# A new order for the mixer steps of a decoder block, other GpSimd work, and 512-column products for w_glu and w_out

## Chip, cores and metric

The kernel runs on one core of one Trainium2 chip. The metric is device time in microseconds (us) from the start to the end of one execution, as the median of several runs. The five engines of the core work from queues of their own, each in its own fixed order: TensorE (PE in the profile; PEld is its weight load), VectorE (DVE), ScalarE (ACT), GpSimd (POOL) and SyncE (SP, which here issues the DMAs).

## What is computed

One layer over 256 positions of 2048 features, batch 1, float32:

```
xn   = rmsnorm(x, norm1_g);  proj = xn @ w_in              # 2048 x 3072
u    = conv4(proj[:, :1024]) ; gate = proj[:, 1024:2048] ; s = proj[:, 2048:]
r, i = sigmoid(u @ w_a + b_a), sigmoid(u @ w_i + b_i)      # 16 heads of 64
a    = exp(-8 r softplus(-lam))
y_rg = gelu(gate) * scan(a, sqrt(1 - a^2) * i * u)         # h_t = a_t h_(t-1) + b_t
z    = gelu(s5(s))            # 64 groups of 16 features, 64 complex states each, a linear scan
y_s5 = z * sigmoid(z @ w_glu + b_glu)                      # 1024 x 1024
x    = x + [rmsnorm(y_rg) ; rmsnorm(y_s5)] @ w_out         # 2048 x 2048
g, v = split(conv3(rmsnorm(x) @ w_up))                     # 2048 x 12288
out  = rmsnorm(x + (gelu(g) * v) @ w_down)                 # 6144 x 2048
```

## The kernel before

Features lie on the 128 partitions and the 256 positions along the free dimension, so each weight matrix is cut into columns of 128 outputs and loads of 512 KB, 128 rows by 8 blocks of 128x128. TensorE multiplies each block with a 128x256 tile of activations.

**Three forms of product.** `product_whole` multiplies the float32 weights as they are; the 24 columns of w_in use it, and the trace shows two matmul instructions of 256 columns for each block. `product` splits every weight into a high and a low part (`part`: a cast on ScalarE, L150, and a subtraction on VectorE, L151) and every activation too (`split`, L198 to 208), and adds three of the four partial products. In its narrow form a block takes three matmuls of 256 columns (L158, L159, L160). In its wide form the two that share the high weights are one matmul of 512 columns (L156) into both halves of a PSUM bank, and `total` afterwards adds the halves: a copy on ScalarE (L166) and an addition on VectorE (L167). The letters in `WIDE` say which products are wide; before it is "FD", which is the feed-forward part except the last output column. The 8 products of w_glu and the 32 half products of w_out, 8 blocks each, are narrow.

**The mixer steps.** `ORDER` is a hand-written list of steps, a letter and an index each, traced in that order:

- U j, P j, B g, G j are the RG-LRU group: product and causal convolution; gates; one batch of four j (exp, tanh, sqrt, and the products of L685 and L686); gate product, scan (L692), gelu and split of the output. P writes its gates into one buffer `tau` per batch, of which there is one.
- S c, T c, K c, N c, Y c, F c, Z c are the S5 group: product; tables of cosines and sines (six instructions, L505 to 507); matrices (six instructions for `ball`, L525 to 527, eight for `cp`, L534 to 538, transposes on TensorE and eight small DMAs issued by SyncE); the scan, some 7 us of VectorE; the output matmuls (L599 to 607); gelu; split.
- W o and E o are the RG half of an output column of w_out and its addition to the residual on GpSimd, L o a column of w_glu, V o the S5 half of w_out with the residual sum, its square (added up on GpSimd) and the split. R, Q and a last call make the three norm factors.

The gate matmuls of P and the output matmuls of Y share one PSUM buffer ("y"). All larger products share four PSUM buffers ("main"), and a buffer of W o is held until E o has read it. Four weight loads (`RAW`) and three split pairs of weights can be in flight.

**Who sets the order on the engines.** The list gives priorities. A planner (`schedule_with_timeline_sim=True`) places every instruction by its own estimates of time, and may take a later step's instruction early when it takes an engine to be free. At run time every engine then follows its own list and waits where an operand is late. The activations that go through `fn` keep the list's order among themselves on ScalarE.

After the mixer come 96 products of w_up and 16 of w_down (6 loads each); neither their code nor their order is edited.

Of the kernel before, what the change touches and what calls it, by code (L numbers as in the profile page):

```python
# [14 lines left out]
P = 128  # L15
D = 2048
# [60 lines left out]
def block_kernel(ctx, tc, a, out):  # L77
# [24 lines left out]
    ADD = V  # L102
    WIDE = "FD"
    WB = 2
# [65 lines left out]
    def product(src, ot, kcs, xs, wide=False):  # L170

        ps = psm.tile([P, 2, T], F32, tag="main", name="ps")
        n = len(kcs) * KC
        j = 0
        for kc in kcs:
            raw = load(src, ot, kc)
            wh, wl = w_parts()
            part(raw, wh, wl)
            for kk in range(KC):
                step(ps, wide, wh, wl, kk, xs[j], j == 0, j == n - 1)  # L180
                j += 1
        flush()
        return ps

# [53 lines left out]

    def add_sq(acc, src, first):
        if first:  # L240
# [41 lines left out]
    with ExitStack() as ph:  # L282
# [207 lines left out]
        for i in range(PB):  # L490
            shapes = ("bp", [P, 2, 4, 32]), ("cp", [P, BL, 2, 4, 32]), ("cb", [P, BL - 1, P]), ("dec", [P, 4, NB])
            pads.append([mix.tile(sh, F32, name=f"{t}{i}") for t, sh in shapes])
            for t in pads[i]:
                G.memset(t, 0.0)

        def s5_tables(c):

            sn_t = mw.tile([P, 4, NB], F32, tag="sn_t", name="sn_t", bufs=TB)
            cs_t = mw.tile([P, 4, NB], F32, tag="cs_t", name="cs_t", bufs=TB)
            t4 = slice(4 * c, 4 * c + 4)  # L500
            xc_, xs4 = (v[:, t4, :NX].unsqueeze(3).to_broadcast([P, 4, NX, NY]) for v in (xc, xs_))
            yc_, ys4 = (v[:, t4, NX:].unsqueeze(2).to_broadcast([P, 4, NX, NY]) for v in (xc, xs_))
            for o, f, g, op in ((cs_t, xc_, xs4, ALU.subtract), (sn_t, xs4, xc_, ALU.add)):
                m = mw.tile([P, 4, NB], F32, tag="tm", name="tm", bufs=1)
                G.tensor_tensor(o.rearrange("p s (a b) -> p s a b", a=NX), f, yc_, ALU.mult)  # L505
                G.tensor_tensor(m.rearrange("p s (a b) -> p s a b", a=NX), g, ys4, ALU.mult)
                G.tensor_tensor(o, o, m, op)
            return cs_t, sn_t

        def s5_mats(c):  # L510
# [12 lines left out]
            for m, (f1, x1, x2_) in enumerate(((fr4, br4, bi4), (nf4, bi4, br4))):  # L523
                m1, m2 = (mw.tile(sh, F32, tag=t, name=t, bufs=1) for t in ("m1", "m2"))
                G.tensor_tensor(m1, x1, f1, ALU.mult)  # L525
                G.tensor_tensor(m2, x2_, fi4, ALU.mult)  # L526
                G.tensor_tensor(ball[:, m].rearrange("p i c k -> p i k c"), m1, m2, ALU.subtract)

# [108 lines left out]
        acc2 = keep("accx")  # L637

        def w_in_col(o):
            return early[o] if o in early else product_whole(a["w_in"], o, (0, 1), xs)  # L640

# [14 lines left out]
        def rg_gates(j):  # L656

            cv, rw = convs[j]
            if j % 4 == 0:
                taus[j // 4] = mix.tile([P, 4, T], F32, tag="tau", name="tau")  # L660
            tau = taus[j // 4]
            pg = ps1.tile([P, 2, T], F32, tag="y", name="pg")
# [5 lines left out]
            G.tensor_tensor(bu[j // 4][:, j % 4, :], ig, cv, ALU.mult)  # L668

        def rg_batch(g):  # L670
# [13 lines left out]
            V.tensor_scalar(a4, q4, -2.0, -1.0, ALU.mult, ALU.add)  # L684
            G.tensor_tensor(b4, b4, q4, ALU.mult)  # L685
            G.tensor_tensor(b4, b4, tau, ALU.mult)  # L686

        def rg_out(j):
# [23 lines left out]
        def s5_split(c):  # L712
            zs[c] = split(cpool, f"x{c}", us[c].rearrange("p b t -> p (b t)"), None)

        def rg_top(o):

            tops[o] = product(a["w_out"], o, (0,), yr, "W" in WIDE)

        def rg_add(o):
            if not xr:  # L720
                for i in range(4):
                    t = keep(f"xq{i}", (P, 4, T))
                    nc.sync.dma_start(t, a["xT"][:, 4 * i:4 * i + 4, :])
                    xr.extend(t[:, k, :] for k in range(4))
                    xq2.append(t)
            u = work.tile([P, T], F32, tag="u", name="u")
            V.tensor_tensor(u, total(tops[o], "W" in WIDE), rs["rg"], ALU.mult)  # L727
            G.tensor_tensor(xr[o], xr[o], u, ALU.add)

        def s5_glu(j):  # L730
            ps = total(product(a["w_glu"], j, (0,), zs, "L" in WIDE), "L" in WIDE)
            sg = work.tile([P, T], F32, tag="cv", name="sg")
            fn(sg, ps, AF.Sigmoid, bias=col("bglu", j))
            ov = work.tile([P, T], F32, tag="rg", name="ov")
            V.tensor_tensor(ov.rearrange("p (t b) -> p b t", b=BL), us[j],
                            sg.rearrange("p (b t) -> p b t", b=BL), ALU.mult)
            add_sq(acc_s5, ov, j == 0)
            tag, n = (("wa", WB), ("wb", WB), ("wx", WB), ("bt", WB))[j % 4]
            ys[j] = split(mw, tag, ov, col("gs5", j), bufs=n)

        def s5_top(o):

            ps = total(product(a["w_out"], o, (1,), ys, "V" in WIDE), "V" in WIDE)
            u = work.tile([P, T], F32, tag="u", name="u")
            V.tensor_tensor(u, ps, rs["s5"], ALU.mult)
            V.tensor_tensor(xr[o], xr[o], u, ALU.add)
            add_sq(acc2, xr[o], o == 0)
            x2[o] = split(cpool, f"x{o}", xr[o], col("g2", o))
# [7 lines left out]
            "Y": lambda c: s5_out(c, outs[c], *mats[c][3:]),  # L756
            "W": rg_top, "E": rg_add, "V": s5_top,
            "R": lambda _: rs.update(rg=rstd([acc_rg], DH, "rstd_rg")),
# [7 lines left out]
    with ExitStack() as ph:  # L766
        hp = ph.enter_context(tc.tile_pool(name="hp", bufs=1))
        hs = []
        hp.tile([P, 16], F32, name="shift")

# [21 lines left out]
        for o in range(KX):  # L792
# [110 lines left out]
```

## Time and profile before

| | us |
|---|---|
| median of 3 runs (1170.81 to 1173.15) | 1171.94 |
| profiled execution: time | 1170.86 |
| profiled execution: span, first to last instruction | 1169.1 |
| TensorE busy in the span | 1141.1 (98%) |
| VectorE, ScalarE, GpSimd busy | 805.2, 574.4, 210.5 |
| mean granted TensorE clock | 0.991 of full |

The span is 1.8 us shorter than the profiled execution's own time. "Busy" counts the time from the start to the modelled end of instructions, so neighbouring instructions overlap by some hundredths of a us, and the distance from one start to the next is the better measure of pace.

### The profile page before, as it was taken

How to read it: one execution, taken by the hardware profiler on the slowest of the kernel's cores; microseconds unless marked ns; L12 is line 12 of the kernel's file. 1: busy time of each engine (PE TensorE's matmuls, PEld its weight loads, DVE VectorE, ACT ScalarE, POOL GpSimd, SP SyncE). 2: the span in 40 equal slices, each digit the busy share in tenths (PEclk: the TensorE clock that was granted, in tenths of full speed). 3: DMA queues.
4: the chain of work that ended last, by engine and by line, in shares of the span. 5: the costliest groups of instructions: out<-in, count | busy, mean ns of one | idle time of the engine just before them, and what ended most of it. 6: DMA issues, size and time to landing. Idle time of an engine off the chain costs nothing.

```text
span 1169.1 us, 19286 instructions
## 1 busy us (share of the span) xinstructions
PE 1141.1 (98%) x7454; PEld 1012.6 (87%) x7454; DVE 805.2 (69%) x1246; ACT 574.4 (49%) x897; POOL 210.5 (18%) x270
## 2 busy tenths in 40 slices
PE   9998979999999999999999999999999999999996
PEld 8787868889998888888888888888888888888886
DVE  7677564567797777878778787778786445444444
ACT  4342522356466555555555555555555444444432
POOL 5898665124240000000000000000000000000000
PEclk9999989999999999999999999999999999999998
DMA  7435435546555666666666666666666666565662
GB/s 274 138 111 164 126 122 158 175 153 181 181 183 181 190 190 190 189 194 185 195 185 196 184 194 186 194 188 190 190 189 192 187 185 193 182 191 185 187 191 92
DMA packets 65980, 209.27 MB, mean 179 GB/s; under 512 B 11872, under 2 KB 15584, under 8 KB 65888
## 3 DMA queue, kind: packets, MB, share of 16 engines
q1 hardware_dynamic: 65744, 207.97, 57.6%
q8 instruction: 58, 0.95, 0.3%
q14 instruction: 34, 0.28, 0.1%
q10 hardware_dynamic: 144, 0.07, 0.0%
HBM read 204.87 MB, written 2.10 MB: 177 GB/s over the span
## 4 chain that ended last, share of the span: by engine, by line
PE 88%; DVE 4%; POOL 4%; DMA 2%; issue 1%; SPq 1%; ACT 1%; DVEq 0%; POOLq 0%; ACTq 0%
PE ps L156 44%; PE ps L160 27%; PE ps L193 6%; PE ps L158 4%; PE ps L159 3%; PE ps L304 2%; PE y L602 1%; DMA raw<-in_w_in 1%; POOL m L525 1%; PE y L607 1%; DMA xq<-in_xT 0%; SPq L561 0%; POOL cp L538 0%; POOL m L526 0%; DVE xq L807 0%
## 5 line engine op out<-in xcount | busy, mean ns | idle before, releaser
L156 PE MATMUL ps<-sp,wh 128*128 128x512 f32 x2256 | 785.5, 392 | 0.0
L160 PE MATMUL ps<-sp,wl 128*128 128x256 f32 x2624 | 738.6, 282 | 0.0
L151 DVE TENSOR_TENSOR wl<-raw,wh 128x1024 fp32r<-128x1024 f32 x328 | 403.8, 1231 | 243.2 <-ACT wh L150 241.8
L150 ACT CAST wh<-raw 128x1024 fp32r<-128x1024 f32 x328 | 344.9, 1052 | 427.2 <-PE ps L156 250.1
L156 PEld LDWEIGHTS ps<-sp,wh 128*128 128x128 f32 x2256 | 422.5, 187 | 94.2
L160 PEld LDWEIGHTS ps<-sp,wl 128*128 128x128 f32 x2624 | 496.8, 189 | 0.0
L245 POOL TENSOR_TENSOR accx<-accx,sq 128x256 f32<-128x256 f32 x29 | 34.9, 1202 | 799.0 <-ACT sq L244 799.0
L193 PE MATMUL ps<-xg,raw 128*128 128x256 f32 x640 | 145.0, 382 | 0.0
L193 PEld LDWEIGHTS ps<-xg,raw 128*128 128x128 f32 x640 | 120.1, 191 | 17.1 <-issue 0.3
L158 PE MATMUL ps<-sp,wh 128*128 128x256 f32 x368 | 104.7, 285 | 1.9 <-DVE u L727 1.9
L159 PE MATMUL ps<-sp,wh 128*128 128x256 f32 x368 | 104.8, 285 | 0.0
L778 DVE SCALAR_TENSOR_TENSOR cv<-u,par,cv 128x255 f32<-128x255 f32 x192 | 92.3, 481 | 4.1 <-ACT cv L776 0.7
L158 PEld LDWEIGHTS ps<-sp,wh 128*128 128x128 f32 x368 | 71.0, 193 | 2.2 <-DVE u L727 2.1
L159 PEld LDWEIGHTS ps<-sp,wh 128*128 128x128 f32 x368 | 71.1, 193 | 0.1
L776 ACT ACTIVATE cv<-u,par 128x256 f32<-128x256 f32 x96 | 57.2, 596 | 0.8 <-DVE u L774 0.8
L774 DVE TENSOR_TENSOR u<-t,rstd 128x256 f32<-128x256 f32 x96 | 40.5, 422 | 1.6
L167 DVE TENSOR_TENSOR t<-t,ps 128x256 f32<-128x256 f32 x96 | 39.8, 414 | 0.0
L166 ACT COPY t<-ps 128x256 f32<-128x256 f32 x96 | 34.7, 361 | 0.0
L304 PE MATMUL ps<-xg,raw 128*128 128x256 f32 x128 | 28.3, 380 | 1.1 <-ACT xg L279 0.9
L304 PEld LDWEIGHTS ps<-xg,raw 128*128 128x128 f32 x128 | 24.1, 190 | 4.9 <-ACT xg L279 1.3
L796 DVE TENSOR_TENSOR xq<-xq,ps 128x256 f32<-128x256 f32 x31 | 13.0, 421 | 16.1 <-PE ps L160 15.6
L538 POOL TENSOR_TENSOR cp<-m,m 64x192 f32<-64x192 f32 x32 | 20.9, 653 | 8.3 <-PE y L607 6.4
(231 smaller groups left out, 696.7 us busy)
## 6 DMA issues: line engine op xcount, KB each, us to landing
raw<-in_w_up SPq DMA_DIRECT2D x192, 512.0 KB, 3.6
raw<-in_w_down SPq DMA_DIRECT2D x96, 512.0 KB, 3.6
raw<-in_w_in SPq DMA_DIRECT2D x47, 512.0 KB, 3.7
raw<-in_w_out SPq DMA_DIRECT2D x32, 512.0 KB, 3.6
raw<-in_w_glu SPq DMA_DIRECT2D x8, 512.0 KB, 3.7
xq<-in_xT SPq DMA_DIRECT2D x7, 512.0 KB, 4.8
out_y<-xq SPq DMA_DIRECT2D x6, 256.0 KB, 2.1
rw<-in_rgw SPq DMA_DIRECT2D x8, 128.0 KB, 3.5
```

The costliest lines, as they stand in the source:

```text
L150: S.copy(wh, raw)
L151: V.tensor_tensor(wl, raw, wh.bitcast(F32), ALU.subtract)
L156: PE.matmul(ps, lhsT=wh[:, kk, :], rhs=x, start=first, stop=False)
L158: PE.matmul(ps[:, 0, :], lhsT=wh[:, kk, :], rhs=x[:, 0, :], start=first, stop=False)
L159: PE.matmul(ps[:, 0, :], lhsT=wh[:, kk, :], rhs=x[:, 1, :], start=False, stop=False)
L160: PE.matmul(ps[:, 0, :], lhsT=wl[:, kk, :], rhs=x[:, 0, :], start=False, stop=last)
L167: V.tensor_tensor(t, t, ps[:, 0, :], ALU.add)
L193: PE.matmul(ps, lhsT=raw[:, kk, :], rhs=x[j], start=j == 0, stop=j == n - 1)
L304: PE.matmul(ps, lhsT=raw0[i][:, k % KC, :], rhs=xs[k], start=k == 0, stop=k == KX - 1)
L774: V.tensor_tensor(u, ps, rs["n2"], ALU.mult)
L776: S.activation(cv, u, AF.Identity, bias=col("fcb", o), scale=col("fcw", 2 * 2 * KF + o))
L778: V.scalar_tensor_tensor(cv[:, d:], u[:, :T - d], col("fcw", (2 - d) * 2 * KF + o), cv[:, d:], ALU.mult, ALU.add)
```

## The change

The list of steps is replaced by another over the same steps. A letter for each index says whether a part runs on VectorE (V) or GpSimd (G); before, all these parts ran on GpSimd: the tables of T (5 of 8 go to VectorE), `ball` of K (4 of 8), `cp` of K (2 of 8), the product of P's gate (1 of 8) and the two products of B (1 of 2). `WIDE` gains W, L and V, so all 40 products of w_glu and w_out take the wide form. The last pair of scaled inputs moves to the buffer of `yr[7]`. The first square of a sum is now found by a list, since steps may start at any index. The other new switches stand at values that change nothing (`WHOLE` lists all 24 columns, `PRENORM` is off, `PG_TAG`, `CB_TAG` and `EADD` name what was there).

```
 ORDER = """
-U0 X0 S0 P0 U1 P1 T0 K0 U2 P2 S1 N0 Y0 U3 P3 B0 T1 K1 U4 P4 S2 N1 Y1 U5 P5 T2 K2 U6 P6 S3 N2 Y2 U7 P7 B1 T3 K3 F0
-F1 F2 G0 S4 N3 Y3 F3 T4 K4 G1 G2 S5 N4 Y4 F4 T5 K5 G3 G4 S6 N5 Y5 F5 T6 K6 G5 G6 S7 N6 Y6 F6 T7 K7 G7 N7 Y7 F7 R0
-W0 Z0 Z1 E0 W1 Z2 Z3 E1 W2 Z4 Z5 E2 W3 Z6 Z7 E3 L0 L1 W4 E4 L2 L3 W5 E5 L4 L5 W6 E6 L6 L7 W7 E7 W8 E8 W9 E9 Q0 W10
-E10 W11 E11 W12 E12 W13 E13 W14 E14 W15 E15 V0 V1 V2 V3 V4 V5 V6 V7 V8 V9 V10 V11 V12 V13 V14 V15
+U2 S0 U0 X0 T0 P0 K0 P2 U1 U4 N0 T1 P1 Y0 U3 S1 K1 P3 B0 S2 N1 P4 Y1 T2 S3 U5 U6 K2 P5 N2 G0 Y2 U7 F2 P7 T3 K3 F1 N3 S4 P6 G2 T4 K4 S7 S5 B1 Y3 F3 G3 K5 N4 T5 F0 T6 Y4 G5 G1 F4 S6 K6 G6 N6 T7 N5 G4 Y6 G7 F6 Y5 K7 Z3 N7 R0 W0 W1 F5 W2 W4 Z4 Y7 Z6 E0 Z1 F7 W3 E1 E2 E3 Z0 Z5 Z7 Z2 L2 L1 E4 W5 L4 L0 E5 W6 E6 L5 L3 L7 L6 W11 E11 W7 E7 W8 W12 Q0 W14 E8 V3 W9 E12 W10 E9 E10 E14 V0 V12 V5 W13 E13 W15 V2 E15 V10 V14 V7 V6 V15 V1 V4 V11 V8 V9 V13
 """
+TABLES = 'VVVVVGGG'
+BALL = 'VGVGGVGV'
+CPOW = 'GGGGVVGG'
+GATED = 'GGGGVGGG'
+BATCH = 'GV'
+WIDTH = 'FDWLV'
-    WIDE = "FD"
+    WIDE = WIDTH
...
         if k % 2 == 0:
-            pair = cpool.tile([P, 2, T], F32, tag=f"x{KH + k // 2}", name="xg")
+            if k < KX - 2:
+                pair = cpool.tile([P, 2, T], F32, tag=f"x{KH + k // 2}", name="xg")
+            else:
+                pair = mix.tile([P, 2, T], F32, tag="y7", name="xg")
...
+        def who(names, c):
+            return G if names[c] == "G" else V
...
+            e = who(TABLES, c)
...
-                G.tensor_tensor(o, o, m, op)
+                e.tensor_tensor(o, o, m, op)
...
-            G.tensor_tensor(b4, b4, q4, ALU.mult)
-            G.tensor_tensor(b4, b4, tau, ALU.mult)
+            who(BATCH, g).tensor_tensor(b4, b4, q4, ALU.mult)
+            who(BATCH, g).tensor_tensor(b4, b4, tau, ALU.mult)
```

(The same replacement of `G` by `e` or `who(...)` stands at the instructions of `ball`, `cp` and the gate product.)

## Rows read from the trace of the kernel before

**Rows 1.** The page: TensorE's busy time, share and instructions.

```profile
PE 1141.1 (98%) x7454; PEld 1012.6 (87%) x7454; DVE 805.2 (69%) x1246; ACT 574.4 (49%) x897; POOL 210.5 (18%) x270
```

**Rows 2.** Windows, stage by stage: stretch, length, each engine's busy us (instructions), clock.

```profile
29.00:230.00 201.00, 187.46 (x1607) 157.60 (x1606) 124.20 (x198) 67.60 (x152) 134.85 (x178) 0.97 0.45 139
...
294.00:353.70 59.70, 59.70 (x500) 59.70 (x499) 52.65 (x71) 33.66 (x51) 19.78 (x20) 1.00 0.57 183
...
365.00:465.00 100.00, 100.00 (x578) 88.15 (x578) 79.64 (x128) 59.17 (x92) 0.00 (x0) 1.00 0.62 190
```

**Rows 3.** Windows around TensorE's four stops in the mixer, same columns.

```profile
44.00:64.00 20.00, 16.66 (x121) 13.23 (x120) 9.64 (x16) 6.11 (x17) 19.40 (x30) 1.00 0.52 164
96.00:104.00 8.00, 4.80 (x77) 3.94 (x76) 4.35 (x6) 1.75 (x5) 6.97 (x8) 0.80 0.01 2
146.00:160.00 14.00, 7.11 (x84) 5.68 (x83) 9.84 (x16) 3.07 (x10) 9.67 (x13) 0.76 0.35 123
244.00:252.00 8.00, 5.82 (x35) 5.45 (x34) 3.47 (x8) 2.27 (x5) 2.79 (x4) 0.79 0.47 155
```

**Rows 4.** Timeline of TensorE: start, us, instruction [idle before, who ended it].

```profile
47.15 0.44 PE L545 MATMUL tp<-par,ball 128*128 128x128 f32 x2 [0.76 <-POOL ball L527]
...
100.37 0.43 PE L599 MATMUL y<-wx,cp 128*32 128x64 f32 x16 [3.20 <-ACT ig L119]
...
153.80 0.44 PE L599 MATMUL y<-wx,cp 128*32 128x64 f32 x8 [6.68 <-DVE wx L588]
...
247.66 0.58 PE L158 MATMUL ps<-sp,wh 128*128 128x256 f32 x1 [1.86 <-DVE u L727]
```

**Rows 5.** Timeline of ScalarE and VectorE: the work that two of these stops waited for.

```profile
99.48 0.47 ACT L119 ACTIVATE tau<-pg,par 128x256 f32<-128x256 f32 x1 [5.58 <-POOL xq L686]
...
148.94 4.22 DVE L692 TENSOR_TENSOR_SCAN xq<-xq,xq 128x256 f32<-128x256 f32 x4
153.08 0.66 DVE L588 TENSOR_TENSOR wx<-wx,wb 128x256 f32<-128x256 f32 x1
```

**Rows 6.** Timeline of TensorE: two wide blocks of the first w_up product.

```profile
353.75 0.40 PE L156 MATMUL ps<-sp,wh 128*128 128x512 f32 x1
...
354.10 0.40 PE L156 MATMUL ps<-sp,wh 128*128 128x512 f32 x1
```

**Rows 7.** Timeline of VectorE: one whole V step, of sixteen.

```profile
331.92 1.23 DVE L151 TENSOR_TENSOR wl<-raw,wh 128x1024 fp32r<-128x1024 f32 x1
333.06 0.97 DVE L208 SCALAR_TENSOR_TENSOR sp<-xq,par,sp 128x256 fp32r<-128x256 f32 x1
333.95 0.41 DVE L745 TENSOR_TENSOR u<-ps,rstd_s 128x256 f32<-128x256 f32 x1
334.40 0.42 DVE L746 TENSOR_TENSOR xq<-xq,u 128x256 f32<-128x256 f32 x1
334.80 1.23 DVE L151 TENSOR_TENSOR wl<-raw,wh 128x1024 fp32r<-128x1024 f32 x1
```

**Rows 8.** Groups of instructions by line: count, busy us, mean ns, idle before.

```profile
L167 DVE TENSOR_TENSOR t<-t,ps 128x256 f32<-128x256 f32 x96 | 39.8, 414 | 0.0
L166 ACT COPY t<-ps 128x256 f32<-128x256 f32 x96 | 34.7, 361 | 0.0
L538 POOL TENSOR_TENSOR cp<-m,m 64x192 f32<-64x192 f32 x32 | 20.9, 653 | 8.3 <-PE y L607 6.4
...
L527 POOL TENSOR_TENSOR ball<-m,m 128x256 f32<-128x256 f32 x16 | 13.4, 836 | 10.9 <-PE tp L545 10.5
...
L507 POOL TENSOR_TENSOR cs_t<-cs_t,tm 128x256 f32<-128x256 f32 x8 | 7.3, 908 | 0.1
...
L686 POOL TENSOR_TENSOR xq<-xq,tau 128x1024 f32<-128x1024 f32 x2 | 5.1, 2570 | 0.0
```

**Rows 9.** VectorE at two lines: shortest, median and longest ns of one.

```profile
L581 DVE TENSOR_TENSOR wa<-wa,wb x8: 412/615/866, 60.6 to 234.2; 128x256 f32<-128x256 f32 x8
...
L208 DVE SCALAR_TENSOR_TENSOR sp<-xq,par,sp x16: 479/964/969, 312.9 to 356.1; 128x256 fp32r<-128x256 f32 x16
```

More of the change, by code (lines that the diff above doesn't have):

```diff
@@ L172, in product, with products @@
         ps = psm.tile([P, 2, T], F32, tag="main", name="ps")
+        products(ps, src, ot, kcs, xs, wide)
+        flush()
+        return ps
+    def products(ps, src, ot, kcs, xs, wide, first=True, last=True):
         n = len(kcs) * KC
@@ L179, in product @@
             for kk in range(KC):
-                step(ps, wide, wh, wl, kk, xs[j], j == 0, j == n - 1)
+                step(ps, wide, wh, wl, kk, xs[j], first and j == 0, last and j == n - 1)
                 j += 1
-        flush()
-        return ps
     def product_whole(src, ot, kcs, x):
@@ L237, in rstd_direct, with add_sq @@
         return r
-    def add_sq(acc, src, first):
-        if first:
+    begun = []
+    def add_sq(acc, src):
+        if not any(acc is b for b in begun):
+            begun.append(acc)
             S.activation(acc, src, AF.Square)
@@ L524, in s5_mats @@
                 m1, m2 = (mw.tile(sh, F32, tag=t, name=t, bufs=1) for t in ("m1", "m2"))
[L525 to L527 removed]
+                e.tensor_tensor(m1, x1, f1, ALU.mult)
+                e.tensor_tensor(m2, x2_, fi4, ALU.mult)
+                e.tensor_tensor(ball[:, m].rearrange("p i c k -> p i k c"), m1, m2, ALU.subtract)
+            e = who(CPOW, c)
             sh = [P, BL - 1, 4, 16]
@@ L637, in block_kernel, with x_split @@
         acc2 = keep("accx")
+        def x_split(k):
+            xp.append(split(cpool, f"x{k}", xs[k], None))
         def w_in_col(o):
-            return early[o] if o in early else product_whole(a["w_in"], o, (0, 1), xs)
+            if o in early:
+                return early[o]
+            if o in WHOLE:
+                return product_whole(a["w_in"], o, (0, 1), xs)
+            return total(product(a["w_in"], o, (0, 1), xp, "I" in WIDE), "I" in WIDE)
         def rg_u(j):
@@ L733, in s5_glu @@
             fn(sg, ps, AF.Sigmoid, bias=col("bglu", j))
-            ov = work.tile([P, T], F32, tag="rg", name="ov")
+            ov = aa[j // 4][:, j % 4, :] if PRENORM else work.tile([P, T], F32, tag="rg", name="ov")
             V.tensor_tensor(ov.rearrange("p (t b) -> p b t", b=BL), us[j],
                             sg.rearrange("p (b t) -> p b t", b=BL), ALU.mult)
-            add_sq(acc_s5, ov, j == 0)
-            tag, n = (("wa", WB), ("wb", WB), ("wx", WB), ("bt", WB))[j % 4]
-            ys[j] = split(mw, tag, ov, col("gs5", j), bufs=n)
+            add_sq(acc_s5, ov)
+            if not PRENORM:
+                ys[j] = split(mw, ("wa", "wb", "wx", "bt")[j % 4], ov, col("gs5", j), bufs=WB)
         def s5_top(o):
[L743 to L747, printed above, removed]
+            if PRENORM:
+                products(tops[o], a["w_out"], o, (1,), ys, "V" in WIDE, first=False)
+                flush()
+                for h in range(1 + ("V" in WIDE)):
+                    V.tensor_tensor(xr[o], xr[o], tops[o][:, h, :], ALU.add)
+            else:
+                ps = total(product(a["w_out"], o, (1,), ys, "V" in WIDE), "V" in WIDE)
+                u = work.tile([P, T], F32, tag="u", name="u")
+                V.tensor_tensor(u, ps, rs["s5"], ALU.mult)
+                V.tensor_tensor(xr[o], xr[o], u, ALU.add)
+            add_sq(acc2, xr[o])
             x2[o] = split(cpool, f"x{o}", xr[o], col("g2", o))
@@ L756, in block_kernel @@
             "Y": lambda c: s5_out(c, outs[c], *mats[c][3:]),
-            "W": rg_top, "E": rg_add, "V": s5_top,
+            "W": rg_top, "V": s5_top, "A": lambda _: [x_split(k) for k in range(KX)],
+            "H": lambda j: PRENORM and rg_normed(j), "I": lambda j: PRENORM and s5_normed(j), "D": lambda _: xr or x_again(), "E": rg_add,
             "R": lambda _: rs.update(rg=rstd([acc_rg], DH, "rstd_rg")),
```

69 lines of the change are left out of this document (47 added, 22 removed).

## The prediction

> **What bounds the kernel now.** I read the page first: TensorE is busy for 98% of the span [rows 1], so whatever the change does on other engines counts only where TensorE stops or slows for it. The windows by stage say where that is [rows 2]: in the feed-forward part (365 to 465 us) and in the stretch of w_glu and w_out (294 to 353.7 us) TensorE is busy without a break at full clock; in the first mixer stretch, 29 to 230 us, it is busy for 187.46 of 201 us at a mean clock of 0.97. So there is something to win in the mixer only.
>
> Windows laid around the gaps in TensorE's timeline find nearly all of it in four places [rows 3]: TensorE idles 3.34 us in 44 to 64, 3.20 in 96 to 104, 6.89 in 146 to 160 and 2.18 in 244 to 252, in sum 15.6 us. Three of these windows also show a clock below full: 0.80, 0.76 and 0.79. With levels of 2.4 and 1.2 GHz that is 2 x 0.20 x 8 = 3.2 us, 2 x 0.24 x 14 = 6.7 us and 2 x 0.21 x 8 = 3.4 us at 1.2 GHz, each begun after a stop; the several short stops of 44 to 64 left the clock at 1.00. Where TensorE works at half clock it loses half of the time: 1.6, 2.5 (it starts again only at 153.8, some 1.8 us into the low clock) and 1.7 us, in sum 5.8. All that this part can give back is 15.6 + 5.8 = 21.4 us.
>
> The timeline with its releasers says what each stop waited for [rows 4]. The first kind (47.15 and three more) is `ball` and `cp`, which GpSimd makes; GpSimd was busy for 19.40 of those 20 us [rows 3]. At 100.37 the output matmuls Y wait for the shared PSUM buffer, which the gates of P hold until ScalarE can write `tau`, and that waited 5.58 us for the last product of the batch B on GpSimd, L686 [rows 5]. At 153.8 Y waits for the result of the scan step N (L588) on VectorE; in front of it in VectorE's queue stood four scans L692 of 4.22 us together [rows 5], work of G that the planner had put there. At 247.66 a W product waits for a PSUM buffer that E frees after the norm factor R [rows 4].
>
> **What the change does, part by part.**
>
> *Work moved from GpSimd to VectorE.* Five of 8 tables are 30 instructions, four of 8 `ball` 24, two of 8 `cp` 16, one gate product, and two of the batch. At the rows' means of 908, 836, 653, 836 and 2570 ns [rows 8] that is 27.2 + 20.1 + 10.4 + 0.8 + 5.1 = 64 us off GpSimd's 134.85 [rows 2]. On VectorE an addition of 128x256 took 412 to 866 ns, median 615 [rows 9], the longer ones beside GpSimd work; for 128x1024 the nearest row is 1.23 us [rows 7]. The 71 small ones and the two large ones thus cost between 29.3 + 2.5 = 32 us and 61.5 + 2.5 = 64 us of VectorE; with GpSimd half as busy I take 0.5 us each, 38 us. VectorE then carries 124 + 38 = 162 us in a stretch that shrinks to 201 - 13.4 = 188 us if TensorE stops nowhere, 86%. It fits, but with less room than before (62%); at the upper end, 188 us, it fits no more.
>
> On this point the Trainium skill, "SBUF — State Buffer", section "Who interferes with whom", says that a VectorE instruction with two SBUF inputs and a GpSimd instruction that reads SBUF exclude each other for the whole instruction. By that rule each moved instruction could wait out a whole GpSimd instruction, some 0.84 us here, which would put the estimate above the upper end; the trace agrees that they hinder each other, but its longest addition lost 0.45 us.
>
> *44 to 64 us* (3.3 us): the first `ball` and the first tables go to VectorE, which was busy for only 9.64 of those 20 us, while GpSimd makes `cp` at the same time. I count 2.5 us back, between 0 and 3.3.
>
> *96 to 104 us* (3.2 + 1.6): B0 stays on GpSimd and P4 still stands between B0 and Y1, so the chain is there; but GpSimd has lost the tables that stood between, so its two products can follow their operands. I count two thirds, 3.2 us, between 0 and 4.8.
>
> *146 to 160 us* (6.9 + 2.5): B1 goes to VectorE, and the steps G that need it now stand far apart in the list, so four scans need not come due at one time. But N keeps its 7 us of VectorE beside more other work. I count half, 4.7 us, between 0 and 9.4.
>
> *244 to 252 us* (2.2 + 1.7): a wide W is first added up by `total`, which needs no norm factor, so PSUM buffers come free before R; two more products can run, and each is 8 blocks, 2.8 us. I count all, 3.9 us, between 2 and 3.9.
>
> *Wide products.* Columns through TensorE stay the same; a matmul instruction goes. From the windows, a narrow block takes 3 x 59.7 / 500 = 0.358 us and a wide one 2 x 100 / 578 = 0.346 us [rows 2]; in the mixer two wide blocks stood 0.35 us apart [rows 6]. That is 0.06 to 0.10 us for a product of 8 blocks. Against it stand a copy of 361 ns on ScalarE and an addition of 414 ns on VectorE for each [rows 8]. ScalarE has room (33.66 of 59.7 us busy). VectorE has it where W's are mixed in, but not in a run of V's: one V step occupied VectorE without a gap for 2.88 us, 331.92 to 334.80 [rows 7], exactly the 8 narrow blocks of TensorE. With the addition, which overlaps its neighbours by some 0.05 us, a V takes about 3.25 us against 2.8 of TensorE: VectorE sets the pace. The new list ends in eleven V's in a row: 11 x 0.37 = 4.0 us lost. If the split (L208) no longer falls beside GpSimd's sum of squares, it takes 479 instead of 964 ns [rows 9] and nothing is lost; without that, and with no overlap, 11 x 0.41 = 4.5. For the 16 W and the 5 other V I count 21 x 0.10 = 2.1 us won (1.3 at the slower pace); the 8 L come out even. The first w_up product needs the residual column of the last V only at its 14th block, 13 x 0.35 = 4.5 us in, which covers that V's epilogue of about 3 us: 0.
>
> *More on VectorE in front.* For stops that the 38 us bring elsewhere I count 2.5 us; the bound is nothing below and, above, one more stop like that at 153.8, 9.4.
>
> *Moved at no cost.* The last inputs' new buffer is needed again only by G7, the last w_in product in the list. The loads keep their number and their queue; K's eight small DMAs stand behind fewer late operands, and four weight loads are ahead of TensorE, at 2.8 us or more each. Gates and gelus now alternate more, so ScalarE changes its tables oftener; it was busy for 67.60 of 201 us and can take that in.
>
> **Sum**, against the profiled execution's 1170.86 us (span 1169.1): -2.5 - 3.2 - 4.7 - 3.9 = -14.3; wide products -2.1 + 4.0 = +1.9; new stops +2.5. Together -9.9, so 1161.0. That execution lies 1.1 us under the median of the runs, 1171.94; as a median I predict 1162.
>
> **Rivals.** A change within 0.2% (2.3 us) is about what a measurement of this kernel can't tell from none.
>
> *R1, all stops go*: VectorE's load at the lower end, 32 us, and no loss in the V's: 1170.9 - 21.4 - 2.1 = 1147.4, as a median 1148.5. For it speaks that no engine but TensorE is near full; against it that N, B and the gates keep their chains. 0.15.
>
> *R2, the list does not do what its parts promise*: the planner fills the queues by its own estimates, puts other ready work before N again, and the stops at 100 and 153.8 come back at other places; then only 44 to 64 and 244 to 252 give 6.4, less the 1.9 of the wide products and 2.5 to 4.5 of new stops: 1171 to 1173 as a median. The four scans in front of L588 show that it happens [rows 5]. 0.19.
>
> *R3, the other sign: VectorE becomes the bound of the first stretch.* The place is the queue in front of N: tables and `ball` of the following steps stand there, Y is late, and TensorE, whose order is fixed, stops and restarts at 1.2 GHz, 9.4 us each time by the third window [rows 3]. It decides from two such stops on: 14.3 - 1.9 - 2 x 9.4 = -6.4, so 1177, as a median 1178. For it speaks the load of 86 to 100%; against it that GpSimd's relief makes VectorE's own instructions shorter. 0.22.
>
> My forecast, 0.44, runs from 1155 to 1168 by itself. Faster takes it, R1 and 0.03 of R2: 0.62. Same takes 0.12 of R2, slower R3 and 0.04 of R2: 0.26. The range of 8 in 10 runs from 1149, the edge of R1, to 1178, the price of R3.
>
> **What would show it.** Right: the four windows' counterparts with less than 6 us of idle TensorE in sum and at most one stretch at 1.2 GHz; VectorE busy for over 80% of the first stretch; V steps of 3.2 us or more in the last run, with TensorE waiting for `wl` there. Wrong: stops of 5 us or more before Y with VectorE as releaser (R3), V steps at 2.8 us, or first w_up matmuls that wait for a late split.

## The result, and the profile after

The changed kernel takes 1152.36 us as a median of four runs (1151.71 to 1153.13), the kernel before 1171.87 (1170.81 to 1173.15) on the same chip: a ratio of 0.9833, 95% interval 0.9816 to 0.985. That is 19.5 us faster, 9.6 us below the forecast and under its own interval (1155 to 1168), and only 3.9 us above rival R1 (1148.5). The profiled execution took 1151.79 us, its span is 1150.0 and its mean granted clock 0.997.

The page and the windows by stage, which answer to [rows 1, 2, 3] (the first split product now starts at 212 instead of 230 us):

```profile
PE 1133.6 (99%) x7134; PEld 987.9 (86%) x7134; DVE 821.4 (71%) x1359; ACT 593.0 (52%) x943; POOL 155.9 (14%) x197
```

```profile
29.00:212.00 183.00, 181.87 (x1517) 153.95 (x1515) 132.50 (x271) 73.48 (x152) 73.26 (x99) 1.00 0.51 153
212.00:230.00 18.00, 15.34 (x188) 12.64 (x187) 12.68 (x21) 10.07 (x20) 4.80 (x7) 1.00 0.56 186
230.00:294.00 64.00, 64.00 (x410) 55.78 (x410) 54.00 (x84) 44.08 (x80) 23.38 (x22) 1.00 0.59 173
294.00:335.00 41.00, 41.00 (x239) 36.14 (x237) 39.12 (x67) 28.83 (x54) 17.34 (x15) 1.00 0.61 182
335.00:345.00 10.00, 9.09 (x51) 7.32 (x50) 7.63 (x13) 3.98 (x7) 2.34 (x2) 1.00 0.67 189
```

TensorE now idles 183 - 181.87 = 1.13 us in the first stretch and 18 - 15.34 = 2.66 in the second, and then not until after 335; no window of these shows a clock below full. Before, it idled 13.54 us from 29 to 230 (the first window of [rows 2]) and 2.18 from 244 to 252 [rows 3], and lost 5.8 at half clock: 21.5 us, of which 3.8 are left. The timeline shows one of the small stops (68.41), the one stop of size (219.33) and one in w_up, and then what 219.33 waited for, on SyncE and GpSimd (it answers to [rows 4]):

```profile
68.41 0.65 PE L626 MATMUL y<-wx,cp 128*32 128x64 f32 x16 [0.74 <-DVE wx L615]
...
219.33 0.37 PE L578 MATMUL cb<-cp,bp 128*32 128x96 f32 x8 [2.66 <-DMA cp<-in_s5p]
...
337.09 0.39 PE L171 MATMUL ps<-sp,wl 128*128 128x256 f32 x1 [0.66 <-DVE wl L162]
...
212.28 0.38 SPq L539 DMA_DIRECT2D cp<-in_s5p  x1
...
216.92 1.58 POOL L565 TENSOR_TENSOR cp<-m,m 64x192 f32<-64x192 f32 x2
```

At 219.33 a matmul of step K7 waits for its matrix `cp`. There are two buffers for it. The one that K7 needs is free only after Y5, and Y5 stands right ahead of K7 in the list: its last matmuls run from 212.17, GpSimd writes the parts of `cp` from 214.1 to 218.5, and TensorE, whose order is fixed, waits for them and the small DMA of K7. The DMA is the last to end: issued at 212.28, it has landed at 219.19.

To see how the gain adds up over stages I take from each trace the start of the first w_up product (the last 2256 wide blocks are w_up and 15 of the 16 columns of w_down, and the first of them is that start), the length of w_up, that of those 15 columns and the span:

| us | start of w_up | w_up | w_down | span |
|---|---|---|---|---|
| before | 353.75 | 533.5 | 252.4 | 1169.1 |
| after | 332.92 | 535.3 | 252.4 | 1150.0 |
| `engines_only` | 339.68 | 533.5 | 252.4 | 1155.5 |
| `order_only` | 348.67 | 543.6 | 252.4 | 1174.7 |
| `wide_only` | 350.09 | 533.6 | 252.4 | 1165.5 |
| `narrow` | 338.24 | 543.6 | 252.4 | 1164.0 |
| `old_order` | 334.79 | 543.4 | 252.4 | 1160.5 |
| `batch_only` | 348.55 | 533.5 | 252.4 | 1164.4 |
| `tables_mats` | 343.08 | 533.5 | 252.4 | 1158.4 |
| `y5_first` | 329.24 | 535.3 | 252.4 | 1146.3 |
| `narrow_nudge` | 337.66 | 533.8 | 252.4 | 1153.7 |
| `y5_nudge` | 328.85 | 535.5 | 252.4 | 1146.5 |
| `all_vector` | 329.70 | 535.2 | 252.4 | 1146.7 |
| `v_narrow` | 334.02 | 543.6 | 252.4 | 1159.9 |

From before to after the start moves by 20.8 us: 17.7 in stops and clock, and a remainder of 3.1, which holds the wide products and whatever else isn't counted. Against that, w_up is 1.8 us longer. The w_up column has two groups of values in it, 533.5 to 535.5 and 543.4 to 543.6, though no kernel differs there: that was not expected, and the last group of experiments is about it. Until then the mixer is judged by the start of w_up. Each row is one execution, and its time can lie some us off the median of its kernel's runs, so differences of a us or two between rows show little by themselves.

### The profile page after: what moved, and what is told of

Read it like the earlier page. It is cut to its first block, busy times and chain, and to the rows that moved or that the text cites. A ratio compares the mean times of both kernels' runs of the same rounds, so it can differ in the third digit from the quotient of the medians.

```text
span 1150.0 us, 18728 instructions
## 1 busy us (share of the span) xinstructions
PE 1133.6 (99%) x7134; PEld 987.9 (86%) x7134; DVE 821.4 (71%) x1359; ACT 593.0 (52%) x943; POOL 155.9 (14%) x197
## 4 chain that ended last, share of the span: by engine, by line
PE 90%; DVE 4%; DMA 2%; issue 1%; SPq 1%; POOL 1%; ACT 1%; DVEq 0%; POOLq 0%; ACTq 0%
PE ps L167 50%; PE ps L171 26%; PE ps L208 9%; PE ps L325 2%; SPq L588 1%; DVE wl L162 1%; DMA raw<-in_w_out 1%; DMA cp<-in_s5p 1%; PE ps L170 0%; PE ps L169 0%; DMA xq<-in_xT 0%; DVE xq L873 0%; PE pg L699 0%; PE y L629 0%; DVE rcv L685 0%
## 5 line engine op out<-in xcount | busy, mean ns | idle before, releaser
L167 PE MATMUL ps<-sp,wh 128*128 128x512 f32 x2576 | 898.0, 394 | 0.0
L167 PEld LDWEIGHTS ps<-sp,wh 128*128 128x128 f32 x2576 | 483.1, 188 | 111.6
L208 PE MATMUL ps<-xg,raw 128*128 128x256 f32 x640 | 144.5, 382 | 0.0
L208 PEld LDWEIGHTS ps<-xg,raw 128*128 128x128 f32 x640 | 119.8, 190 | 16.9
L178 DVE TENSOR_TENSOR t<-t,ps 128x256 f32<-128x256 f32 x136 | 56.0, 414 | 0.0
L177 ACT COPY t<-ps 128x256 f32<-128x256 f32 x136 | 49.3, 365 | 1.4 <-DVE u L786 1.4
L787 POOL TENSOR_TENSOR xq<-xq,u 128x256 f32<-128x256 f32 x16 | 19.0, 1193 | 46.8 <-DVE u L786 32.8
L854 DVE TENSOR_TENSOR hv<-ge,cv 128x256 f32<-128x256 f32 x48 | 20.4, 426 | 2.1 <-ACT ge L130 0.4
L130 ACT ACTIVATE ge<-cv 128x256 f32<-128x256 f32 x48 | 20.2, 422 | 0.0
L685 DVE SCALAR_TENSOR_TENSOR rcv<-u,par,rcv 128x255 f32<-128x255 f32 (+2 forms) x24 | 14.3, 605 | 8.1 <-ACT rcv L683 7.8
```

The lines of the kernel that those rows point to most:

```text
L130: ins = S.activation(out, src, func, **kw).ins
L167: PE.matmul(ps, lhsT=wh[:, kk, :], rhs=x, start=first, stop=False)
L177: S.copy(t, ps[:, 1, :])
L178: V.tensor_tensor(t, t, ps[:, 0, :], ALU.add)
L208: PE.matmul(ps, lhsT=raw[:, kk, :], rhs=x[j], start=j == 0, stop=j == n - 1)
```

## The experiments

All kernels are made from the changed one, so all have the new buffer of the last inputs; switches at `G` put a part back on GpSimd. Times are medians; ratios are to the kernel before, run on the same chip, with 95% intervals.

### One part at a time

`engines_only`, the old list and narrow products with the new engines:

```
-ORDER = (the new list), WIDTH = 'FDWLV'
+ORDER = (the list of before), WIDTH = 'FD'
```

> The changed kernel with the old list and the old widths, so only the parts moved from GpSimd to VectorE. T1: -2.5 (44 to 64 us), -3.2 (96 to 104) and, B1 being on VectorE, about half of 4.7 (146 to 160): about 1164 us. T2: the stops come from the list, so 1170 to 1173 us, perhaps slower since VectorE has more to do.

Measured: 1156.77 us, ratio 0.9879 (0.9864 to 0.9894); w_up starts 14.1 us earlier than before. The windows of [rows 3], in this kernel:

```profile
44.00:64.00 20.00, 20.00 (x141) 17.22 (x140) 13.59 (x31) 8.50 (x20) 15.68 (x21) 1.00 0.63 197
96.00:104.00 8.00, 7.15 (x120) 5.45 (x119) 6.59 (x11) 2.13 (x6) 5.83 (x10) 1.00 0.47 145
146.00:160.00 14.00, 13.55 (x153) 11.28 (x152) 12.14 (x25) 3.63 (x10) 11.91 (x15) 1.00 0.59 206
```

The first is full, the others have 0.85 and 0.45 us of stops left where there were 3.20 and 6.89, and the clock doesn't fall there. Neither expectation held: the gain is twice that of T1. With the work moved, the old list can stay and these stops still go.

`order_only`, the new list with all parts on GpSimd and narrow products:

```
+TABLES = BALL = CPOW = GATED = 'GGGGGGGG'; BATCH = 'GG'; WIDTH = 'FD'
```

> The changed kernel with the old engines (all moved parts back on GpSimd) and the old widths (FD), so of the change only the list of steps (and the new buffer of the last inputs). T1, the prediction's parts: the list alone does not unload GpSimd, so the stop at 44 to 64 us stays and of the others only half of the one at 146 to 160 goes: -4.7, about 1167 us. T2, the list alone spaces the chains so that TensorE stops nowhere: all but the 2 us of the wide products, about 1155 us.

Measured: 1172.63 us over ten runs (1170.17 to 1176.56), ratio 1.0014 (1.0001 to 1.0027), where both expectations had a gain. In the profiled execution the start of w_up comes 5.1 us earlier, and its w_up is one of the long ones; but this is the slowest of the ten, 3.9 us over their median, so 5.1 is what one run shows of the list and not its usual worth. ScalarE's timeline shows the chain of [rows 5] again, longer than before: the gates wait 9.99 us (5.58 before) for the batch on GpSimd, which is busy for 7.86 of the 8 us from 96 to 104, and TensorE stops 2.40 us for them at 102.14.

```profile
101.25 0.47 ACT L130 ACTIVATE tau<-pg,par 128x256 f32<-128x256 f32 x1 [9.99 <-POOL xq L721]
```

Two stops for `cp` (2.35 us at 56.98, 2.51 at 229.78) and one of 1.55 us for the gates at 81.78 stand beside it. But the largest stop of the kernel before, the one of 146 to 160 us, is gone with the list alone, although all these parts are still on GpSimd: TensorE has no stop over 0.2 us between 102.14 and 229.78. The windows of the two places:

```profile
96.00:104.00 8.00, 5.60 (x64) 4.65 (x66) 2.75 (x3) 0.84 (x2) 7.86 (x7) 0.97 0.32 82
146.00:160.00 14.00, 14.00 (x81) 12.03 (x80) 6.59 (x9) 13.06 (x23) 7.75 (x12) 1.00 0.57 180
```

`wide_only`, the old list and the old engines with wide products:

```
+ORDER = (the list of before); all letters 'G'; WIDTH = 'FDWLV' stays
```

> The changed kernel with the old list and the old engines, so only the 40 wide products. T1 as predicted: -3.9 (no stop at 244 to 252), -2.4 for W and L at TensorE's pace, +0.37 for each of 16 V's in a row = +5.9: about 1171.5. The same with the V pace of 2.93 us that the changed kernel's profile shows: +0.05 x 16 = 0.8 in place of 5.9, about 1166.5. T2: the widths are worth 2 us at most, 1170 us.

Measured: 1171.07 us over ten runs, ratio 0.9997 (0.9969 to 1.0025); but the runs fall into two groups, five from 1165.62 to 1167.51 and five from 1174.63 to 1177.00. The profiled execution (1167.29) is of the lower one, which the second figure of T1 (1166.5) fits. Its start of w_up is 3.7 us earlier. Of the stop at 247.66 in [rows 4] a part remains:

```profile
253.83 0.47 PE L170 MATMUL ps<-sp,wh 128*128 128x512 f32 x1 [1.25 <-DVE t L181]
```

1.25 us of idle time instead of 2.18, and no half clock after it (4.75 busy of 6.00 us at 1.00 in the window 252 to 258).

`narrow`, list and engines without the widths, and `old_order`, engines and widths without the list:

```
narrow:     +WIDTH = 'FD'
old_order:  +ORDER = (the list of before)
```

> The changed kernel with the old widths: new list and new engines, 40 narrow products. T1 with the V pace of 2.93 us: the widths give 3.9 (buffers free before R) and about 2 (pace of TensorE), so about 1158 us and a stop of some 2 us after R. T2: only the 2 us of pace, about 1154 us. If V's at 3.25 us had cost what the prediction says, it would be 1150 us or less.

> The changed kernel with the old list; new engines and new widths stay. By the first four runs' starts of the feed-forward part (engines alone 14.1 us earlier, widths alone 3.7 earlier, list alone 5.1 earlier) T1, the parts add up: 17.8 us earlier than before, so 1154 us if the w_up part takes 533.5 us, 1164 us if it takes 543.6. T2, the list is needed by the other two: 1160 us or more even with w_up at 533.5.

Measured: `narrow` 1165.48 us, ratio 0.9949 (0.9934 to 0.9963). `old_order` 1162.11, ratio 0.9892 (0.9851 to 0.9933): three runs from 1161.90 to 1162.59, and one of 1152.13; T1, with either length of w_up, was 2 us too high. Both profiled executions have the long w_up. By the start of w_up, `narrow` is 15.5 us ahead of before and `old_order` 19.0: on top of engines and widths the list is worth 1.9 us there. In time even that is in doubt, since the changed kernel's w_up is 1.8 us longer than the short one of before, and the one fast run of `old_order` (1152.13) is as fast as the changed kernel (1152.36). `narrow` has no stop near R, with narrow products: the new list alone removes it. It keeps the stop of K7, here 3.26 us, and has a half clock after it (window by stage):

```profile
212.00:230.00 18.00, 14.74 (x187) 13.91 (x187) 11.12 (x19) 8.72 (x17) 4.81 (x7) 0.91 0.48 169
```

### Which of the moved parts

`batch_only` and `tables_mats` have the old list and narrow products, and divide the moved parts:

```
batch_only:   all letters 'G' but +BATCH = 'GV'
tables_mats:  new letters but +BATCH = 'GG'
```

> Old list, old widths, and of the engines only the second batch's two products (B1) on VectorE; all else on GpSimd as before. T1: the batch on GpSimd makes the stop at 146 to 160 us (it delays the scans that stand before L588): that stop goes, -9.4 at most, 1162 to 1165 us, and the stops at 44 to 64 and 96 to 104 stay. T2: the four scans in VectorE's queue make it and stay there: the stop stays, 1170 to 1172 us.

> Old list, old widths, the new engines for tables, ball, cp and the gate, but both batches on GpSimd. T1: the stops at 44 to 64 (3.3) and 96 to 104 (3.2 + 1.6) go, the one at 146 to 160 stays in part: 1163 to 1167 us. T2, the batch counts for nothing and unloading GpSimd is all: 1157 to 1159 us, as with all engines.

Measured: `batch_only` 1165.13 us, ratio 0.9937 (0.9922 to 0.9951), start of w_up 5.2 earlier. `tables_mats` 1161.36, ratio 0.9910 (0.9894 to 0.9927), 10.7 earlier. Together 15.9, and `engines_only` has 14.1. T1 of `batch_only` held; `tables_mats` came out between its two. The Y stop of 153.8 and the work of TensorE that stands ahead of it, first in the kernel before (the stop itself is in [rows 4]):

```profile
140.77 0.54 PE L551 MATMUL cb<-cp,bp 128*32 128x96 f32 x16
141.24 5.88 PE L193 MATMUL ps<-xg,raw 128*128 128x256 f32 x26
```

then in `batch_only` (TensorE, then VectorE):

```profile
142.16 0.54 PE L581 MATMUL cb<-cp,bp 128*32 128x96 f32 x16
142.63 8.47 PE L211 MATMUL ps<-xg,raw 128*128 128x256 f32 x38
152.99 0.32 PE L629 MATMUL y<-wx,cp 128*32 128x64 f32 x8 [1.89 <-DVE wx L618]
...
147.06 2.43 DVE L730 TENSOR_TENSOR_SCAN xq<-xq,xq 128x256 f32<-128x256 f32 x4
```

in `tables_mats`:

```profile
135.20 0.54 PE L581 MATMUL cb<-cp,bp 128*32 128x96 f32 x16
135.66 8.47 PE L211 MATMUL ps<-xg,raw 128*128 128x256 f32 x38
147.55 0.32 PE L629 MATMUL y<-wx,cp 128*32 128x64 f32 x8 [3.42 <-DVE wx L618]
...
141.74 2.40 DVE L730 TENSOR_TENSOR_SCAN xq<-xq,xq 128x256 f32<-128x256 f32 x4
```

and in `engines_only`:

```profile
135.63 0.54 PE L581 MATMUL cb<-cp,bp 128*32 128x96 f32 x16
136.10 11.06 PE L211 MATMUL ps<-xg,raw 128*128 128x256 f32 x50
147.59 0.65 PE L629 MATMUL y<-wx,cp 128*32 128x64 f32 x16 [0.44 <-DVE wx L618]
```

In all three, four scans still stand together in front of Y's operand, but take 2.4 us instead of 4.22. That is the smaller part of what happened to the stop of 6.68 us. Counted from the start of the matmuls into `cb`, Y begins after 13.03 us in the kernel before and after 10.83, 12.35 and 11.96 us in these three, so its operand came only 2.2, 0.7 and 1.1 us sooner. The rest is TensorE's own list: between `cb` and Y it has 26 w_in matmuls before, 38 in `batch_only` and `tables_mats` and 50 in `engines_only`, which fill 2.6, 2.6 and 5.2 us more of the wait. The list of steps is the same in all four; the planner, which sees other engines, places Y later among the w_in matmuls. (Counted from the start, 498 w_in matmuls stand ahead of Y in the kernel before, then 510, 510 and 522.) No run holds TensorE's order fixed, so what the shorter scans would give by themselves is not shown. The stops of 44 to 64 and 96 to 104 go with the tables and matrices alone: `batch_only` keeps both to a hundredth (16.66 of 20 us busy, 4.81 of 8), `tables_mats` has the 20.00 and 7.15 of `engines_only`.

### The one stop left, and VectorE as the bound

`y5_first` takes N5, Y5 and K7 ahead of N6, G7 and Y6, so that other work of TensorE stands between Y5 and the moment when K7's matrix is ready:

```
-G6 N6 T7 N5 G4 Y6 G7 F6 Y5 K7
+G6 N5 T7 N6 G4 Y5 K7 G7 Y6 F6
```

> The changed kernel with one edit in its list: N5, Y5 and K7 stand before G7 and Y6, so that the matrices of K7 have their buffer a w_in product earlier. T1: the changed kernel's one stop left (2.66 us at 219, before cb) goes, 1149.5 to 1150 us with w_up at 535. T2: the planner lays everything anew, another stop takes its place or w_up takes its other pace: 1152 us or more.

Measured: 1148.12 us (1148.01 to 1148.40), ratio 0.9793 (0.9778 to 0.9808). It is faster than both kernels, by 4.2 us than the changed one (whose interval, 0.9816 to 0.985, lies apart); w_up starts 3.7 us earlier, the 2.66 of the stop and 1.0 that these windows don't explain. Y5 now runs at 200.2, GpSimd writes `cp` from 202.4 to 208.3, and 26 matmuls of w_in fill TensorE until K7's first at 208.44, which waits for nothing. Its windows, the first stretch and the place of the stop:

```profile
29.00:213.00 184.00, 182.88 (x1581) 154.24 (x1580) 134.24 (x272) 75.06 (x156) 79.30 (x105) 1.00 0.51 153
213.00:230.00 17.00, 16.96 (x187) 14.50 (x185) 14.78 (x27) 11.01 (x19) 4.77 (x4) 1.00 0.58 191
```

`all_vector` is `y5_first` with every switched part on VectorE:

```
+TABLES = BALL = CPOW = GATED = 'VVVVVVVV'; BATCH = 'VV'
```

> The kernel of y5_first with all tables, ball, cp, gate and batch products on VectorE, none on GpSimd. T1, VectorE at its shortest durations (about 0.41 us an instruction) has room for them, 72% to about 85% of the first stretch: the front stays, 1148 to 1151 us. R3 of the prediction, VectorE becomes the bound: stops before Y with VectorE as releaser, 1155 us or more.

Measured: 1147.70 us (1146.68 to 1148.46), ratio 0.9794 (0.9779 to 0.9809), the same as `y5_first`. Its first stretch:

```profile
29.00:213.00 184.00, 182.83 (x1595) 155.34 (x1597) 153.36 (x371) 74.51 (x154) 4.37 (x6) 1.00 0.51 155
```

GpSimd does 4.37 us there, VectorE 153.36 of 184 (83%), and TensorE still stops for 1.17 us in sum. Beside `y5_first`, 75 us of GpSimd's work became 99 instructions and 19.1 us of VectorE's busy time, and cost no time: TensorE idles for 1.85 us from 29 to 230 us (1.16 in `y5_first`), no stop over 0.7.

`v_narrow` makes the S5 half of w_out narrow again:

```
+WIDTH = 'FDWL'
```

> The changed kernel with V narrow again (W, L and the feed-forward part wide). If the run of V's had cost what the prediction says (VectorE at 3.25 us a V, +0.37 for each of 11), it is 4 us faster, about 1148 us. If a wide V takes 2.93 us of VectorE as the profile after shows, it makes no difference: 1151 to 1153 us. Either figure with 8 us more if w_up takes its slow rhythm.

Measured: 1162.30 us, ratio 0.9920 (0.9905 to 0.9936), with the long w_up. Its w_up starts at 334.0, 1.1 us later than in the changed kernel, although its stop for `cb` is 1.44 us and not 2.66: wide V's don't hold TensorE up before w_up.

### The two lengths of w_up

`narrow_nudge` is `narrow`, and `y5_nudge` is `y5_first`, with one small matmul repeated in the norm factor that w_up's results wait for (it stands some blocks into w_up), which writes the same values again:

```
-        for h in range(2):
+        for h in (0, 1, 0) if tag == "rstd1" else (0, 1):
             PE.matmul(b[:, P * h:P * h + P], lhsT=s[:, h:h + 1].to_broadcast([P, P]), rhs=ident, ...)
```

> The kernel of narrow with one matmul of the last norm factor (n2) issued a third time, with the same values into the same place; it stands in the break between the first w_up blocks. T1, TensorE has two rhythms for the same stream and the last break before w_up picks one: w_up may take 533.5 us in place of 543.6, then 1155 us, in some runs or in all. T2, the slow w_up follows from what the other engines do in this kernel: 543.6 in every run, 1165 us.

> The kernel of y5_first with the same third matmul of n2. T1: the break picks anew, so 1148 us or some 8 us more, 1156, in some or all runs. T2: as y5_first, 1148 us in every run.

Measured: `narrow_nudge` 1154.78 us, ratio 0.9852 (0.9834 to 0.9869), all of its runs from 1153.75 to 1155.50: 10.7 us under `narrow`, from one more matmul (T1). `y5_nudge` 1148.21, ratio 0.9799 (0.9784 to 0.9813): nothing changes where w_up is short already. The wide matmuls by line (shortest, median and longest ns) in the same 100 us of w_up, first `narrow`:

```profile
L167 PE MATMUL ps<-sp,wh x284: 395/398/403, 399.9 to 499.9; 128*128 128x512 f32 x142
```

then `narrow_nudge`:

```profile
L167 PE MATMUL ps<-sp,wh x290: 391/391/391, 399.6 to 499.8; 128*128 128x512 f32 x145
```

Both are busy for 100.00 of the 100 us at a clock of 1.00, with the same instructions, and the second gets 2% more of them done. In the timelines a block takes 346.7 ns in the short w_up and 353.3 in the long, as a steady pattern. In these two kernels it starts 25 blocks into w_up, where the norm factor's matmuls stand; up to there both run at the long pace. Over the other 1510 of the 1536 blocks 6.6 ns make 10.0 us.

## Why the prediction was right, and where it was not

**The sign and the place were right, the size was not**: the gain is in the mixer's stops, TensorE is busy elsewhere as before, and most of it comes with the work moved off GpSimd (14.1 of 20.8 us at the start of w_up, in `engines_only`). R2 (same time; its own sum gives 1170 to 1172, a us less than I wrote) and R3 (slower) did not happen. R1, with 0.15, came 3.9 us near and my forecast, with 0.44, 9.6: nearly all stops went. Of the three signs that I named for "right" only the first held, less than 6 us of idle TensorE in sum and no stretch at 1.2 GHz; VectorE is busy for 72% and not over 80%, and a V takes 2.93 us and not 3.2. One sign of "wrong" is there, the w_up matmul at 337.09 that waits for its split weights. In the profiled execution the forecast's -9.9 became -19.1 us: 6.1 more in stops, 5.0 more in the products, and 1.8 lost in w_up, of which the sum had nothing.

**The stops were under-counted: the larger of the two terms that made the forecast too high.** I counted 14.3 us back of 21.4 and 2.5 of new stops. Measured: of 21.5 only 1.13 of small stops remain, 20.4 back, and one new stop of 2.66. That the new stop has the size I gave is luck: I meant stops that VectorE's 38 us would bring, and this one comes from the list, K7 right behind Y5 with two buffers for `cp`, under "moved at no cost" in my account. The 6 us are in the gains: two thirds at 96 to 104 and half at 146 to 160. The step that failed is "N keeps its 7 us of VectorE beside more other work. I count half". `engines_only` keeps the old list and has 0.45 us of stops left there, and `order_only` keeps GpSimd's work and has none: either part of the change is enough by itself. I had reckoned with one cure, scans that come due apart, and they don't: in `order_only` and in the changed kernel the four still run in a row (164.6 and 150.88 us), without a stop of TensorE. The runs show others: with the old list the scans take 2.4 us instead of 4.22 where GpSimd is relieved, so their length was itself a result of GpSimd's work, and the planner, given other engines, puts 12 or 24 more w_in matmuls of TensorE ahead of Y, the larger part of the gain. I had priced the stop as if TensorE's own order stayed. At 96 to 104 us both are seen again: the batch's last product starts 3.3 us earlier in `engines_only` (93.86 against 97.11), and 6 more w_in matmuls stand ahead of Y.

**VectorE's load: predicted 162 us of 188 (86%), measured 132.5 of 183 (72%).** The window has 73 instructions more than that of [rows 2] and only 8.3 us more of busy time. (F5, F7 and Y7 now come after R, so a few instructions are not in it; but `engines_only`, with the old list, has 129.91 in the same 183 us.) What was missing in my sum is what VectorE's own instructions gain while GpSimd falls from 134.85 to 73.26 us (by 61.6, where I had 64). Lines of VectorE that were not moved (shortest, median, longest ns of one), in the kernel before:

```profile
L650 DVE SCALAR_TENSOR_TENSOR rcv<-u,par,rcv x24: 457/722/2452, 32.9 to 120.1; 128x255 f32<-128x255 f32 x8, 128x254 f32<-128x254 f32 x8, 128x253 f32<-128x253 f32 x8
```

and after:

```profile
L685 DVE SCALAR_TENSOR_TENSOR rcv<-u,par,rcv x24: 467/486/884, 38.0 to 120.2; 128x255 f32<-128x255 f32 x8, 128x254 f32<-128x254 f32 x8, 128x253 f32<-128x253 f32 x8
...
L608 DVE TENSOR_TENSOR wa<-wa,wb x8: 417/732/815, 61.2 to 216.4; 128x256 f32<-128x256 f32 x8
...
L223 DVE SCALAR_TENSOR_TENSOR sp<-xq,par,sp x16: 472/640/964, 285.7 to 341.0; 128x256 fp32r<-128x256 f32 x16
```

The convolution's median falls from 722 to 486 ns. Not every line gains: L608, the first line of [rows 9] under its new number, has a higher median than before (732 against 615). In `all_vector`, where GpSimd does next to nothing in this stretch, the same line is at its shortest throughout:

```profile
L608 DVE TENSOR_TENSOR wa<-wa,wb x8: 411/418/421, 64.4 to 217.7; 128x256 f32<-128x256 f32 x8
```

So its longer times come with GpSimd's work. I had named this in the argument against R3, and left it out of the sum.

The Trainium skill, "SBUF — State Buffer", section "Who interferes with whom", has the rule of exclusion that I weighed against the change: moved instructions would wait for GpSimd's. The traces agree that the two hinder each other, but the rule works for the change as well, since each instruction moved is one less on GpSimd for all others of VectorE to wait for; `all_vector` shows that end: L608 above, and 153.36 / 371 = 413 ns for the mean instruction of VectorE, the moved ones among them, against 124.20 / 198 = 627 before (of another mix).

**R3 was far away.** Even at 83% of VectorE no stop is over 0.7 us, and the time is the same. The point from which it would decide was not reached by any kernel here.

**The V run: predicted +4.0, measured about even.** VectorE in the last V's (answers to [rows 7]):

```profile
314.89 1.22 DVE L162 TENSOR_TENSOR wl<-raw,wh 128x1024 fp32r<-128x1024 f32 x1
316.03 0.41 DVE L178 TENSOR_TENSOR t<-t,ps 128x256 f32<-128x256 f32 x1
316.36 1.54 DVE L223 SCALAR_TENSOR_TENSOR sp<-xq,par,sp 128x256 fp32r<-128x256 f32 x2
...
318.15 1.22 DVE L162 TENSOR_TENSOR wl<-raw,wh 128x1024 fp32r<-128x1024 f32 x1
...
320.75 1.22 DVE L162 TENSOR_TENSOR wl<-raw,wh 128x1024 fp32r<-128x1024 f32 x1
```

Two V's take 320.75 - 314.89 = 5.86 us, 2.93 each, where I had 3.25. VectorE is the slower one, as predicted, but by 0.16 us a V, and a lead of split weights takes it in: TensorE keeps its 346.7 ns until 337.09, where it waits 0.66 us for `wl`, in w_up and not in the V's. I had named the case in which nothing is lost, the shorter split, without giving it a share: L223's median is 640 ns where L208 of [rows 9] had 964. Of the 1.8 us by which w_up is longer, the 0.66 is such a debt of the V's; even if all of it is, it stands against the 1.1 us that `v_narrow` is later before w_up in spite of a shorter stop, so the wide V's cost 0.7 us at most. In sum the remainder of 3.1 us, V's included, stands where I had 2.1 won and 4.0 lost.

**The stop at 247.66: gone as counted, for part of the reason.** I said that `total` frees PSUM before R. `wide_only` still stops there for 1.25 us; `narrow` does not, with no `total` in W. Wide products shorten it and spare the half clock (2.6 of 3.9), the list removes it whole.

**The list: it removes the stop that I credited it with, in another way, and was not needed for it.** By itself it takes away the stop at 146 to 160 and the one near R, brings others, and moves the start of w_up by 5.1 us in the one execution profiled. On top of the rest it is worth 1.9 by the start and nothing that can be told in time; it brings its own stop at 219, which `y5_first` removes by moving a few steps. With that, it is worth 5.6 by the start.

**w_up was taken as fixed, and is not.** The changed kernel and the one before both have the short one, so the forecast was not touched, which is luck: 10 us more would have put the result at the forecast for no reason in it. But it made `order_only`, `narrow`, `v_narrow` and `old_order` look 10 us worse than their mixers are. By the ratios the three parts alone make 0.14% slower, 1.21% faster and 0.03% faster, which doesn't add up to the 1.67% of the whole; by the start of w_up they make 5.1 + 14.1 + 3.7 = 22.9 us against 20.8, list and engines taking away some of the same stops.

## What to carry to other kernels

When GpSimd is busy beside VectorE, price a move between them by both: here 62 us less of GpSimd's busy time in the first stretch cost VectorE 8 us, because its own instructions got shorter, and a queue of long instructions in front of a late operand may be long only for that reason. Where a planner lays the queues, a stop can also shrink because other work now stands ahead of it: count the instructions in front of the waiting one before crediting its operand. When an order written by hand shares two buffers between steps, look for the reader that stands just ahead of the next writer: moving a few steps gave 4.2 us. And before a time is read as the worth of an edit, compare the stages that the edit does not touch.

## What the runs showed of the hardware that was not expected

**Two rhythms of TensorE for one stream.** Some 1500 blocks of w_up in a row ran at 346.7 or at 353.3 ns each, at full clock and with no wait on another engine. What sets them apart is not the first blocks: `narrow` and `narrow_nudge` both start w_up at the long pace (350, 360, 350 ns and 350, 361, 349 ns from block to block). After 25 blocks stands a break, in which the norm factor's matmuls run (four in the trace, six with the repeated one), and from the third block behind it on `narrow_nudge` keeps the short pace:

```profile
347.39 0.61 PE L238 MATMUL rb<-par,rs 128*128 128x128 f32 x4
...
349.02 0.40 PE L167 MATMUL ps<-sp,wh 128*128 128x512 f32 x1
...
349.37 0.40 PE L167 MATMUL ps<-sp,wh 128*128 128x512 f32 x1
...
349.73 0.40 PE L167 MATMUL ps<-sp,wh 128*128 128x512 f32 x1
```

is `narrow`, and `narrow_nudge` is

```profile
346.82 0.83 PE L238 MATMUL rb<-par,rs 128*128 128x128 f32 x6
...
348.66 0.39 PE L167 MATMUL ps<-sp,wh 128*128 128x512 f32 x1
...
349.00 0.39 PE L167 MATMUL ps<-sp,wh 128*128 128x512 f32 x1
...
349.35 0.39 PE L167 MATMUL ps<-sp,wh 128*128 128x512 f32 x1
```

Starts are 0.35 and 0.36 us apart in the first, 0.34 and 0.35 in the second. By its times the same kernel can take either from run to run (`wide_only` five and five, `old_order` three and one), so it is not a property of the program alone. What decides it is open. One repeated matmul turned it in all runs of `narrow_nudge`, which shows that the break matters and not how; nor is it the only such place, since in `y5_nudge` the long pace goes on behind the break and gives way to the short one seven blocks later, where two matmuls of 512 columns stand one behind the other. The 15 columns of w_down ran at the same 252.4 us in every kernel.

**The clock after a stop.** Stops of like length differ in what follows: after 2.46 us in `narrow_nudge` and 2.51 in `order_only` TensorE ran at 1.2 GHz for 3.4 us, after 2.66 in the changed kernel it stayed at 2.4; of two stops of 0.32 and 1.86 us near R, the one of before was followed by 1.2 GHz and that of `engines_only` was not. Nor does the low clock always last as long: after the stop near 100 us it lasted 3.4 us in the kernel before (3.20 us of stop) and 6.8 us in `wide_only` and `batch_only` (3.21 and 3.19). In these kernels the length of a stop alone did not tell what the clock would do; 3.4 us at 1.2 GHz with TensorE at work cost 1.7 us more.
